# A joint inverse of the 16-blocks by doubling, one block to a partition, with roots and beta products on VectorE

## The chip, the core and the metric

The kernel runs on one core of a Trainium2 chip. The metric is the device time of one execution in microseconds (us). The engines are called by the profile's names: PE (TensorE; PEld is its weight load), DVE (VectorE), ACT (ScalarE), POOL (GpSimd) and SP, whose queue issues the transfers (DMA) spoken of here. Each engine executes its instructions in the order in which they were placed on it.

## What is computed

One inference step of a hybrid recurrent decoder of one layer, for 1024 prompt tokens and 8 x 4 sample tokens, in fp32. Cut to what matters:

```
h = RMSNorm(x);  z = h @ w_in
A: gated DeltaNet   o = delta rule over chunks of 64: solve (I + L) sol = rhs, L strictly lower
                    y = o * rsqrt(mean(o*o) + eps) * g * silu(z)
B: RWKV-7           S_t = S_t-1 diag(w) + (S_t-1 (-kk)) (kk*a)^T + v k^T,  o_t = S_t r_t
                    y = group_norm(o) + bonus, times a gate
C: Griffin RG-LRU
x = x + sum_b(sigmoid(gate_b) * (y_b @ w_branch[b])) @ w_out
x = x + relu(RMSNorm(x) @ w_up)^2 @ w_down;   final RMSNorm
```

Both recurrences of A and B are computed in chunks of 64 tokens. Each chunk needs the inverse of a unit triangular 64x64 matrix. It is built from the inverses of its four diagonal 16x16 blocks, then of 32x32, then of 64x64 blocks.

## The kernel before

**Stages.** From the start to about 360 us the first projections run, from there to about 1300 us the middle stage, then the branches are merged and the last GEMMs run. All large products (GEMMs) are computed in three passes of a high and a low half, in `mm3` (lines L306, L307, L308), 352 tokens at a time. Their weights come by 256 KB loads on SP (L291); ACT makes the high half whi (L296), and in the middle stage POOL makes the low half wlo (L297).

**The loop of the middle stage.** Eighteen turns (L1305 to L1325), nine segments for each of two halves of the heads. A turn has a part of branch B, the generator `rwkv_seg` (ur), and one of branch A, `gdn_seg` (ug), and is pipelined by one turn: `next(ur)` prepares B's chunk (decays, reciprocal, the products BK of beta times k, GM from BK and AR); `tri` inverts the matrices of the turn before; `chain` runs the products that use them, and ends with the norms; `next(ug)` prepares A's matrix LA (L1208); `inv16` inverts the 16-blocks. The projections and gates of later columns are in the same program, and a static scheduler, which runs when the program is built, interleaves everything into one order for each engine. GEMMs lie in PE's order between the small matmuls of the loop.

**inv16 (L771 to L794).** It treats six 64x64 matrices together (nt = 6, four of GM, two of LA; four in the turns with B's sample segment). Eight DMAs write the diagonal blocks of GM to DRAM (L781), eight those of LA (L782), a block's row being 64 bytes. One load (L784) brings them back as i16b, each group's blocks repeated on 16 partitions: 128 partitions of 1536 numbers, 768 KB. Then DVE runs fifteen steps of a column recurrence, each a product (L792) and a reduction (L793). The result u16 lies with the rows on the partitions, as `tri` needs it. POOL copies the unit columns in advance (L789, L790).

**tri (L802).** It spreads u16 into ixt (L799), transposes it (L820, tile ix), and begins its matmuls with L824.

**The roots.** `rsqrt` (L579) computes 1/sqrt by a guess on the bits and three Newton steps: on V (DVE) 10 operations, on P (POOL) 13. The root of branch B's group norm (tiles nwyr, nwtr, called at L1110, used on DVE at L1111) and that of branch A's norm (nwyo, nwto, called at L1288, used on ACT at L1291 to scale oa) are on POOL. The one of the q/k norms (nwyg) is on DVE.

**Beta products.** BK's two halves, from kk and from zk, are made by L962: kk's two operations on POOL, zk's two on DVE.

Of the kernel before, what the change touches and what calls it, by code (L numbers as in the profile page):

```python
# [366 lines left out]
def build(tc, ap):  # L367
    nc = tc.nc
    with ExitStack() as ctx:
        k = K(tc, ctx, ap)  # L370
# [208 lines left out]
        def rsqrt(x, shape, tag, E):  # L579

            yi = k.tile(mp, shape, "nwy" + tag, 2, I32)
            t = k.tile(mp, shape, "nwt" + tag, 1)
            E.tensor_scalar(out=yi, in0=x.bitcast(I32), scalar1=-0.5, scalar2=1597463007.0, op0=ALU.mult, op1=ALU.add)
            y = yi.bitcast(F32)
            for _ in range(3):
                E.tensor_tensor(out=t, in0=y, in1=y, op=ALU.mult)
                if E is V:
                    E.scalar_tensor_tensor(out=t, in0=t, scalar=-0.5, in1=x, op0=ALU.mult, op1=ALU.mult)
                    E.scalar_tensor_tensor(out=y, in0=t, scalar=1.5, in1=y, op0=ALU.add, op1=ALU.mult)
                else:  # L590
                    E.tensor_tensor(out=t, in0=t, in1=x, op=ALU.mult)
                    E.tensor_scalar(out=t, in0=t, scalar1=-0.5, scalar2=1.5, op0=ALU.mult, op1=ALU.add)
                    E.tensor_tensor(out=y, in0=t, in1=y, op=ALU.mult)
            return y
# [176 lines left out]
        def inv16(J):  # L771
# [3 lines left out]
            dr = tc.dram_tile([128, nt, 16], F32, name=f"scr_i{k.n}")
            for g in range(8):
                x = slice(16 * g, 16 * g + 16)
                q = 16 * (g % 4)  # L780
                S.dma_start(dr[x, 0:nb], GM[x, g // 4, 0:nb, q:q + 16])  # L781
                S.dma_start(dr[x, nb:nt], LA[x, :, 0, 16 * g:16 * g + 16])  # L782
            mb = k.tile(mp, [128, 1536], "i16b", 1)[:, :256 * nt]
            S.dma_start(mb, dr.rearrange("(g k) b c -> g (k b c)", k=16).unsqueeze(1).to_broadcast([8, 16, 256 * nt]))  # L784
            mb = mb.rearrange("p (k b c) -> p k b c", k=16, b=nt)
            e16 = k.c("e16").unsqueeze(1).to_broadcast([128, nt, 16])
# [735 lines left out]
```

## Time and profile before

| | |
|---|---|
| median of 3 runs | 2380.67 us (2380.59 to 2381.06) |
| profiled execution | 2385.66 us |
| its span, first to last instruction | 2383.9 us |
| mean granted clock of TensorE, share of full speed | 0.937 |
| PE busy in the span | 2225.8 us (93%) |
| DVE, ACT, POOL busy | 1214.3, 814.5, 467.2 us |

The times that follow are those of the profiled execution, counted from the start of its span. The granted clock is a share of 2.4 GHz; 0.50 is the lower level, 1.2 GHz. "Idle before" is the time in which an engine had nothing under way ahead of an instruction, and the name behind it is what ended that time. A turn is counted by when its LA is inverted, from 0.

### The profile page before, as it was taken

How to read it: one execution, taken by the hardware profiler on the slowest of the kernel's cores; microseconds unless marked ns; L12 is line 12 of the kernel's file. 1: busy time of each engine (PE TensorE's matmuls, PEld its weight loads, DVE VectorE, ACT ScalarE, POOL GpSimd, SP SyncE). 2: the span in 40 equal slices, each digit the busy share in tenths (PEclk: the TensorE clock that was granted, in tenths of full speed). 3: DMA queues.
4: the chain of work that ended last, by engine and by line, in shares of the span. 5: the costliest groups of instructions: out<-in, count | busy, mean ns of one | idle time of the engine just before them, and what ended most of it. 6: DMA issues, size and time to landing. Idle time of an engine off the chain costs nothing.

```text
span 2383.9 us, 43121 instructions
## 1 busy us (share of the span) xinstructions
PE 2225.8 (93%) x16939; PEld 2077.3 (87%) x16939; DVE 1214.3 (51%) x2904; ACT 814.5 (34%) x1917; POOL 467.2 (20%) x979
## 2 busy tenths in 40 slices
PE   8999998889888988888978999999999999999997
PEld 7988997678777776777768999999999999999997
DVE  7454347566666675665542037656343333433437
ACT  6465344333433433343322221344122121221234
POOL 3013232432334334223322200032000000000003
PEclk9999998788988897898889999999999999999999
DMA  4213333232323243223223354431111111111114
GB/s 139 71 55 113 102 106 103 80 80 71 88 73 103 67 112 85 78 73 82 68 74 105 121 172 160 158 96 63 45 45 45 49 46 48 45 47 43 49 47 151
DMA packets 149011, 200.15 MB, mean 84 GB/s; under 512 B 36676, under 2 KB 89284, under 8 KB 148808
## 3 DMA queue, kind: packets, MB, share of 16 engines
q1 hardware_dynamic: 148808, 197.40, 27.5%
q8 instruction: 133, 2.18, 0.4%
q14 instruction: 70, 0.57, 0.1%
HBM read 152.61 MB, written 44.72 MB: 83 GB/s over the span
## 4 chain that ended last, share of the span: by engine, by line
PE 55%; DVE 5%; POOL 4%; issue 2%; DMA 2%; ACT 1%; SPq 0%; DVEq 0%; POOLq 0%; ACTq 0%
PE g L306 16%; PE g L307 16%; PE g L308 16%; DVE i16t L792 1%; DMA i16b<-scr_i 1%; PE sr L1041 1%; DVE i16u L793 1%; PE rr L976 1%; POOL wlo L297 0%; PE rg L1204 0%; POOL BK L962 0%; PE sr L1116 0%; DVE ahi L1502 0%; PE sg L1238 0%; PE rr L824 0%
## 5 line engine op out<-in xcount | busy, mean ns | idle before, releaser
L306 PE MATMUL g<-hhi,whi 128*128 128x352 f32 x2568 | 861.8, 336 | 7.7 <-DVE z L360 7.1
L308 PE MATMUL g<-hhi,wlo 128*128 128x352 f32 x2568 | 858.6, 334 | 1.7 <-POOL wlo L297 1.7
L307 PE MATMUL g<-hlo,whi 128*128 128x352 f32 x2472 | 828.8, 335 | 2.6 <-DVE hlo L499 1.6
L306 PEld LDWEIGHTS g<-hhi,whi 128*128 128x128 f32 x2568 | 499.6, 195 | 16.9 <-DVE z L360 8.3
L308 PEld LDWEIGHTS g<-hhi,wlo 128*128 128x128 f32 x2568 | 499.5, 195 | 10.1 <-issue 2.3
L307 PEld LDWEIGHTS g<-hlo,whi 128*128 128x128 f32 x2472 | 482.0, 195 | 11.3 <-DVE hlo L499 2.7
L296 ACT CAST whi<-wraw 128x512 fp32r<-128x512 f32 x326 | 201.2, 619 | 522.5 <-PE g L307 498.7
L308 PE MATMUL g<-ahi,wlo 128*128 128x352 f32 x768 | 248.4, 323 | 0.0
L306 PE MATMUL g<-ahi,whi 128*128 128x352 f32 x768 | 248.4, 323 | 0.0
L307 PE MATMUL g<-alo,whi 128*128 128x352 f32 x768 | 248.1, 323 | 0.0
L297 DVE TENSOR_TENSOR wlo<-wraw,whi 128x512 fp32r<-128x512 f32 x216 | 151.4, 701 | 163.5 <-ACT whi L296 158.6
L297 POOL TENSOR_TENSOR wlo<-wraw,whi 128x512 fp32r<-128x512 f32 x110 | 148.4, 1350 | 349.4 <-ACT whi L296 332.3
L1423 POOL TENSOR_TENSOR acc<-acc,sq 128x352 f32<-128x352 f32 x36 | 36.9, 1026 | 910.5 <-ACT sq L1422 744.6
L1484 DVE TENSOR_TENSOR x<-g,x 128x352 f32<-128x352 f32 x192 | 100.4, 524 | 201.1 <-PE g L308 201.1
L308 PEld LDWEIGHTS g<-ahi,wlo 128*128 128x128 f32 x768 | 144.8, 189 | 0.1
L306 PEld LDWEIGHTS g<-ahi,whi 128*128 128x128 f32 x768 | 144.6, 188 | 0.2
L307 PEld LDWEIGHTS g<-alo,whi 128*128 128x128 f32 x768 | 144.6, 188 | 0.1
L1473 DVE TENSOR_TENSOR rl<-rl,g 128x352 f32<-128x352 f32 x96 | 49.8, 519 | 131.0 <-ACT rl L1472 131.0
L792 DVE TENSOR_TENSOR i16t<-i16u,i16b 128x6 f32<-128x6 f32 (+5 forms) x270 | 84.2, 312 | 28.6 <-DMA i16b<-scr_i 21.7
L1472 ACT ACTIVATE rl<-g 128x352 f32<-128x352 f32 x96 | 44.4, 463 | 136.2 <-PE g L308 136.2
L1475 DVE TENSOR_TENSOR alo<-rl,ahi 128x352 fp32r<-128x352 f32 x96 | 50.4, 525 | 47.5 <-ACT ahi L1474 47.5
L1356 ACT ACTIVATE z<-g 128x352 f32<-128x352 f32 x72 | 33.3, 463 | 111.5 <-PE g L308 111.0
(361 smaller groups left out, 2995.1 us busy)
## 6 DMA issues: line engine op xcount, KB each, us to landing
wraw<-win SPq DMA_DIRECT2D x126, 256.0 KB
wraw<-wdn SPq DMA_DIRECT2D x80, 256.0 KB
wraw<-wup SPq DMA_DIRECT2D x64, 256.0 KB
scr_t<-z SPq DMA_DIRECT2D x24, 528.0 KB
tgl<-scr_t SPq DMA_DIRECT2D x24, 528.0 KB
i16b<-scr_i SPq DMA_DIRECT2D x16, 768.0 KB
scr_za<-z SPq DMA_DIRECT2D x16, 528.0 KB
wraw<-wout SPq DMA_DIRECT2D x32, 256.0 KB
```

The source lines that it names most:

```text
L296: self.A.copy(hi, r3)
L297: self.lo_eng.tensor_tensor(out=lo, in0=r3, in1=hi.bitcast(F32), op=ALU.subtract)
L306: T.matmul(ps, whi(k), xhi(k), start=start and k == ks[0], stop=False)
L307: T.matmul(ps, whi(k), xlo(k), start=False, stop=False)
L308: T.matmul(ps, wlo(k), xhi(k), start=False, stop=stop and k == ks[-1])
L792: V.tensor_tensor(out=t[:, :, 0:c], in0=u[:, :, 0:c], in1=mb[:, 0:c, :, c].rearrange("p k b -> p b k"), op=ALU.mult)
L1356: A.activation(out=tz[:, gl(g)], in_=ps, func=AF.Tanh, scale=0.5)
L1423: (V if last else P).tensor_tensor(out=acc[g], in0=acc[g], in1=sq, op=ALU.add)
L1472: A.activation(out=rl, in_=ps, func=AF.Relu)
L1473: V.tensor_tensor(out=rl, in0=rl, in1=ps, op=ALU.mult)
L1475: V.tensor_tensor(out=b[:, gl(g)], in0=rl, in1=a[:, gl(g)].bitcast(F32), op=ALU.subtract)
L1484: V.tensor_tensor(out=x2[c][:, gl(g)], in0=ps, in1=x2[c][:, gl(g)], op=ALU.add)
```

## The change

**The inverse.** `inv16` becomes two functions. `inv16_load` writes the diagonal 64x64 blocks whole, with two DMAs for GM and two for LA, into one DRAM tile whose blocks are 64 x 64 + 64 numbers apart; so the 16x16 diagonal blocks lie at one stride and one load fetches them: 48 partitions (8 nt), one block of 256 numbers to a partition, in runs of 64 bytes. `inv16_solve` inverts all blocks at once by doubling: unit diagonal, then 2x2, 4x4, 8x8, 16x16, where each step fills the corner R between two inverted blocks with a11 M a22, on DVE, in 17 operations. Its result Z is written to DRAM (one DMA) and read back as u16 (two DMAs), in the layout that `tri` reads. POOL sets Z to the unit matrix ahead of it.

**The roots and products.** `rsqrt` loses its POOL form; every root is ten operations on DVE. Both halves of BK are on DVE, four operations.

```diff
-        def rsqrt(x, shape, tag, E):
+        def rsqrt(x, shape, tag):
...
-                E.tensor_tensor(out=t, in0=y, in1=y, op=ALU.mult)
-                if E is V:
-                    E.scalar_tensor_tensor(out=t, in0=t, scalar=-0.5, in1=x, op0=ALU.mult, op1=ALU.mult)
...
+                V.tensor_tensor(out=t, in0=y, in1=y, op=ALU.mult)
+                V.scalar_tensor_tensor(out=t, in0=t, scalar=-0.5, in1=x, op0=ALU.mult, op1=ALU.mult)
+                V.scalar_tensor_tensor(out=y, in0=t, scalar=1.5, in1=y, op0=ALU.add, op1=ALU.mult)
...
-            for g in range(8):
-                x = slice(16 * g, 16 * g + 16)
-                q = 16 * (g % 4)
-                S.dma_start(dr[x, 0:nb], GM[x, g // 4, 0:nb, q:q + 16])
-                S.dma_start(dr[x, nb:nt], LA[x, :, 0, 16 * g:16 * g + 16])
-            mb = k.tile(mp, [128, 1536], "i16b", 1)[:, :256 * nt]
-            S.dma_start(mb, dr.rearrange("(g k) b c -> g (k b c)", k=16).unsqueeze(1).to_broadcast([8, 16, 256 * nt]))
...
+            w = 64 * 64 + 64
+            dr = tc.dram_tile([2 * nt * w], F32, name=f"scr_i{k.n}")
+            for h in range(2):
+                d = dr[h * nt * w:(h + 1) * nt * w].rearrange("(b x) -> b x", b=nt)[:, 0:64 * 64].rearrange("b (p t) -> p b t", t=64)
+                S.dma_start(d[:, 0:nb], GM[H[h], h, 0:nb, 0:64])
+                S.dma_start(d[:, nb:nt], LA[H[h], :, 0, 64 * h:64 * h + 64])
+            M = J["M"] = k.tile(mp, [48, 272], "i16m", 1)[:8 * nt]
+            src = dr.rearrange("(g x) -> g x", g=8 * nt)[:, 0:16 * 64].rearrange("g (k t) -> g k t", t=64)[:, :, 0:16]
+            S.dma_start(M[:, 0:256], src)
+
+        def inv16_solve(J):
...
+            P.memset(Z, 0.0)
+            P.memset(Z[:, 0:272:17], 1.0)
...
+            V.tensor_copy(Z[:, 1:256:34], M[:, 1:256:34])
...
+            V.tensor_copy(R_, blocks(M, 2, 0, 2))
+            V.tensor_tensor(out=t2, in0=R_[:, :, :, 0], in1=a22.unsqueeze(2).to_broadcast([r, 4, 2]), op=ALU.mult)
+            V.tensor_tensor(out=R_[:, :, :, 1], in0=R_[:, :, :, 1], in1=t2, op=ALU.add)
+            V.tensor_tensor(out=t2, in0=R_[:, :, 1], in1=a11.unsqueeze(2).to_broadcast([r, 4, 2]), op=ALU.mult)
+            V.tensor_tensor(out=R_[:, :, 0], in0=R_[:, :, 0], in1=t2, op=ALU.add)
+
+            def product(out, a, b, n):
...
+                for i in range(m):
+                    V.tensor_tensor(out=p_[:, i], in0=a[:, i].unsqueeze(2).to_broadcast([r, n, n, n]),
+                                    in1=b[:, i].rearrange("p k c -> p c k").unsqueeze(1).to_broadcast([r, n, n, n]), op=ALU.mult)
+                if len(out.shape) == 2:
+                    V.tensor_reduce(out=out, in_=pr_[:, :m * n * n * n].rearrange("p (x k) -> p x k", k=n), axis=AXX, op=ALU.add)
+                    return
+                for i in range(m):
+                    V.tensor_reduce(out=out[:, i], in_=p_[:, i], axis=AXX, op=ALU.add)
+
+            for n in (4, 8):
+                t = tt[:, :8 * n]
+                product(t, blocks(M, n, 0, n), blocks(Z, n, n, n), n)
+                product(blocks(Z, n, 0, n), blocks(Z, n, 0, 0), t.rearrange("p (i r c) -> p i r c", r=n, c=n), n)
+            k.n += 1
+            dr = tc.dram_tile([2, nt, 64, 16], F32, name=f"scr_i{k.n}")
+            S.dma_start(dr.rearrange("h b (q k) c -> (h b q) (k c)", q=4), Z[:, 0:256])
             u = k.tile(mp, [128, 6, 16], "i16u", 2)[:, :nt]
-            t = k.tile(mp, [128, 6, 16], "i16t", 2)[:, :nt]
-            P.tensor_copy(u[:, :, 0:1], e16[:, :, 0:1])
-            P.tensor_copy(t, e16)
-            for c in range(1, 16):
-                V.tensor_tensor(out=t[:, :, 0:c], in0=u[:, :, 0:c], in1=mb[:, 0:c, :, c].rearrange("p k b -> p b k"), op=ALU.mult)
-                V.tensor_reduce(out=u[:, :, c], in_=t[:, :, 0:c + 1], axis=AXX, op=ALU.add)
+            for h in range(2):
+                S.dma_start(u[H[h]], dr[h].rearrange("b p c -> p b c"))
...
-                for src, j, e in ((kk, 0, P), (zk, 1, V)):
+                for src, j, e in ((kk, 0, V), (zk, 1, V)):
...
-                rs = rsqrt(mv[:, 1], [128, nb], "r", P)
+                rs = rsqrt(mv[:, 1], [128, nb], "r")
...
-                rs = rsqrt(oss[:n, :nb], [n, nb], "o", P)
+                rs = rsqrt(oss[:n, :nb], [n, nb], "o")
...
-            inv16(J)
+            inv16_load(J)
+            inv16_solve(J)
```

Lines of the kernel after that are spoken of: the way there is L776, L777 and L780, the solve L792 and L803 to L820, the way back L828 and L831; the root's operations are still L583 to L588, ixt is L837, BK L1000, GM L1017, and L1111 and L1293 of before are L1149 and L1331.

**The order on DVE, turn 12.** Before, behind the reciprocal: k L1111 takes the group norm's root nwyr from POOL, then come the last of B's preparation and the first recurrence steps (i16t, i16u), with gtm and GM between them.

```order
L955 RECIPROCAL k_1653_10550<-k_1653_10550 128x256
L964 TENSOR_TENSOR zr_10518<-zr_10518,par 128x256
L1111 TENSOR_TENSOR k_1596_10255<-k_1596_10255,nwyr_10322 128x256
L1293 SCALAR_TENSOR_TENSOR zg_9895<-sg_10510,d_hang,zg_9895 128x256
L956 TENSOR_TENSOR k_1652_10549<-k_1652_10549,k_1653_10550 128x256
L959 TENSOR_TENSOR zk_10519<-zk_10519,WA_10528 128x256
L962 TENSOR_TENSOR BK_10527<-zk_10519,k_1650_10544 64x4x64 x2
L1120 TENSOR_TENSOR k_1608_10347<-k_1608_10347,zv_9582 128x256
L965 TENSOR_TENSOR zr_10518<-zr_10518,zk_10519 128x256
L792 TENSOR_TENSOR i16t_10432<-i16u_10431,i16b_10429 128x6
L1241 SCALAR_TENSOR_TENSOR gtm_10942<-sg_10944,sc,kv_10365 128x128
L793 TENSOR_REDUCE i16u_10431<-i16t_10432 128x6
```

After, at the same place on DVE, the first half of the solve (i16z, i16t) stands among the operations of the two roots (nwto, nwyo, nwtr, nwyr), ahead of the reciprocal.

```order
L1147 TENSOR_SCALAR mv_10021<-mv_10021 128x4
L792 COPY i16z_10122<-i16m_10120 48x8
L803 COPY i16z_10122<-i16m_10120 48x4x2x2
L583 TENSOR_SCALAR nwyr_10028<-mv_10021 128x4
L587 SCALAR_TENSOR_TENSOR nwto_10180<-nwto_10180,oss_10150 128x2
L804 TENSOR_TENSOR i16t_10126<-i16z_10122 48x8
L586 TENSOR_TENSOR nwtr_10029<-nwyr_10028 128x4
L588 SCALAR_TENSOR_TENSOR nwyo_10179<-nwto_10180,nwyo_10179 128x2
L805 TENSOR_TENSOR i16z_10122<-i16z_10122,i16t_10126 48x4x2
```

Further on, still on DVE after, the end of the solve and what stands between it and ixt.

```order
L814 TENSOR_TENSOR i16p_10125<-i16z_10122,i16t_10126 48x512
L997 TENSOR_TENSOR zk_10200<-zk_10200,WA_10209 128x256
L820 TENSOR_REDUCE i16z_10122<-i16p_10125 48x8x8
L1000 TENSOR_TENSOR BK_10208<-k_1691_10230,k_1689_10225 64x4x64 x2
L1000 TENSOR_TENSOR BK_10208<-zk_10200,k_1689_10225 64x4x64 x2
L1002 TENSOR_TENSOR zr_10199<-zr_10199,par 128x256
L1279 SCALAR_TENSOR_TENSOR gtm_10601<-sg_10603,sc,kv_10068 128x128
L1003 TENSOR_TENSOR zr_10199<-zr_10199,zk_10200 128x256
L1279 SCALAR_TENSOR_TENSOR gtm_10601<-sg_10603,sc,kv_10068 128x128
L1017 TENSOR_TENSOR GM_10256<-rr_10257,con 128x512
L1017 TENSOR_TENSOR GM_10256<-rr_10258,con 128x512
L837 TENSOR_TENSOR ixt_10276<-i16u_10146,con 128x192
```

The solve moved ahead of BK and GM, and these moved between its end and ixt; no operation waits for POOL's nwyr or nwyo any more.

**The order on SP's queue, turn 12.** Before: the eight writes of LA, loads of other parts of the turn, one weight load, and the broadcast i16b.

```order
L782 DMA scr_i_10412<-LA_10364 16x2x16 x8
L1167 DMA gr_11302<-scr_g 128x128 x2
L291 DMA wraw_13855<-win 128x512
L784 DMA i16b_10429<-scr_i_10412 128x1x1536
L902 DMA ll_10998<-scr_l 128x2x128
```

After: the two writes of LA (L777) are followed by one weight load and a load of gr; then come the load i16m, other loads, the stores of both norms' results (scr_y), the write of Z (i16z) and its read (i16u).

```order
L780 DMA i16m_10120<-scr_i_10115 48x16x16
L1205 DMA gr_10955<-scr_g 128x128
L1398 DMA scr_t<-z_13306 128x1056
L291 DMA wraw_13583<-win 128x512
L940 DMA ll_10654<-scr_l 128x2x128
L938 DMA zv_10201<-scr_zb_91 128x2x128
L1161 DMA scr_y<-k_1644_10050 128x128 x2
L1334 DMA scr_y<-zg_9623 128x128 x2
L1211 DMA kq_10958<-scr_za_93 128x2x128 x2
L828 DMA scr_i_10144<-i16z_10122 48x256
L1213 DMA zg_10511<-scr_za_93 128x2x128
L831 DMA i16u_10146<-scr_i_10144 64x6x16 x2
```

The queue has one more round trip in each turn, and its last part stands behind the stores of the norms' results.

**The order on PE.** Between the first and the last of tri's first matmuls (L824, after L862) PE's order holds 1885 GEMM matmuls (L306 to L308) before and 1981 after, of 10584 in both.

## Rows read from the trace of the kernel before

**Rows 1.** windows: length; PE, PEld, DVE, ACT, POOL busy (count); clock; DMA
```profile
360.00:1300.00 940.00, 819.63 (x8321) 693.00 (x8320) 564.78 (x1782) 339.52 (x1048) 307.41 (x759) 0.86 0.31 84
1300.00:2384.00 1084.00, 1064.52 (x6614) 1059.90 (x6612) 469.99 (x829) 292.07 (x549) 69.54 (x61) 0.99 0.25 80
```

**Rows 2.** waits of PE from 360 to 1300 us (total, times, longest)
```profile
PE sg L1292 <- ACT oa L1291: 40.8, 16, 4.9
PE sr L1116 <- DVE k L1111: 25.9, 12, 5.3
PE rr L824 <- DVE ix L820: 23.2, 9, 5.6
```

**Rows 3.** tri's first matmul, line L824 (ns min/median/max, first and last start)
```profile
L824 PE MATMUL rr<-ix,GM x544: 184/191/258, 390.8 to 1253.7; 32*32 32x32 f32 x182
```

**Rows 4.** timeline of DVE, turn 12 (start, duration, operation, idle before)
```profile
973.26 0.47 DVE L1208 SCALAR_TENSOR_TENSOR LA<-rg,gsl,ar 128x256 f32<-128x256 f32 x1
...
981.00 0.17 DVE L1109 TENSOR_SCALAR mv<-mv 128x4 f32<-128x4 f32 x1
981.08 1.74 DVE L955 RECIPROCAL k<-k 128x256 f32<-128x256 f32 x1
...
989.32 0.43 DVE L1111 TENSOR_TENSOR k<-k,nwyr 128x256 f32<-128x256 f32 x1 [6.22 <-POOL nwyr L593]
...
1004.87 0.32 DVE L792 TENSOR_TENSOR i16t<-i16u,i16b 128x90 f32<-128x90 f32 x1
...
1005.51 0.36 DVE L799 TENSOR_TENSOR ixt<-i16u,con 128x192 f32<-128x192 f32 x1
```

**Rows 5.** timeline of POOL, turn 12: where the first root begins
```profile
980.55 0.19 POOL L583 TENSOR_SCALAR nwyo<-oss 128x2 int32<-128x2 int32 x1
```

**Rows 6.** timeline of PE, turn 12
```profile
989.89 1.12 PE L1116 MATMUL sr<-con,k 64*64 64x64 f32 x16 [3.71 <-DVE k L1111]
...
1007.94 0.45 PE L824 MATMUL rr<-ix,GM 32*32 32x32 f32 x32
```

**Rows 7.** windows, the stretch behind PE's stop in turn 12
```profile
985.90:1003.00 17.10, 13.39 (x74) 11.79 (x73) 10.52 (x34) 2.39 (x6) 5.22 (x13) 0.50 0.34 85
```

**Rows 8.** timeline of DVE, turn 13
```profile
1022.03 0.87 DVE L1208 SCALAR_TENSOR_TENSOR LA<-rg,gsl,ar 128x256 f32<-128x256 f32 x2
...
1028.18 1.75 DVE L955 RECIPROCAL k<-k 128x256 f32<-128x256 f32 x1
...
1068.33 0.87 DVE L1208 SCALAR_TENSOR_TENSOR LA<-rg,gsl,ar 128x256 f32<-128x256 f32 x2
```

**Rows 9.** timeline of PE, turn 13
```profile
1050.81 0.65 PE L824 MATMUL rr<-ix,GM 32*32 32x32 f32 x32 [2.01 <-DVE ix L820]
```

**Rows 10.** timeline of SP's queue, first turn
```profile
368.49 0.67 SPq L784 DMA_DIRECT2D i16b<-scr_i  x1
```

**Rows 11.** timeline of DVE, first turn
```profile
378.85 0.17 DVE L792 TENSOR_TENSOR i16t<-i16u,i16b 128x6 f32<-128x6 f32 x1 [2.94 <-DMA i16b<-scr_i]
```

**Rows 12.** chain that ended last: two loads in it (start, duration)
```profile
943.64 2.41 DMA zk<-scr_zb
...
1034.38 3.05 DMA kq<-scr_za
```

**Rows 13.** groups of instructions by form (count; busy us, mean ns; idle before)
```profile
L976 PE MATMUL rr<-AR,BK 64*128 64x128 f32 x272 | 50.2, 354 | 10.9 <-POOL BK L962 9.8 <-ACT og L970 1.1
...
L962 DVE TENSOR_TENSOR BK<-zk,k 64x256 f32<-64x256 f32 x32 | 22.8, 714 | 0.7
...
L979 DVE TENSOR_TENSOR GM<-rr,con 128x512 f32<-128x512 f32 x32 | 21.8, 685 | 14.2 <-PE rr L976 14.2
...
L586 DVE TENSOR_TENSOR nwtg<-nwyg 128x2 f32<-128x2 f32 x48 | 8.4, 175 | 1.0
...
L963 DVE TENSOR_TENSOR AR<-zr,k 128x256 f32<-128x256 f32 x16 | 7.8, 484 | 0.4 <-ACT k L936 0.4
...
L1104 DVE TENSOR_REDUCE mv<-k 128x4 f32<-128x256 f32 x16 | 6.5, 409 | 0.0
```

More of the change, by code (lines that the diff above doesn't have):

```diff
@@ L577, in b4 @@
             return a.rearrange("p (b w) -> p b w", b=NB)
-        def rsqrt(x, shape, tag, E):
+        def rsqrt(x, shape, tag):
             yi = k.tile(mp, shape, "nwy" + tag, 2, I32)
             t = k.tile(mp, shape, "nwt" + tag, 1)
-            E.tensor_scalar(out=yi, in0=x.bitcast(I32), scalar1=-0.5, scalar2=1597463007.0, op0=ALU.mult, op1=ALU.add)
+            V.tensor_scalar(out=yi, in0=x.bitcast(I32), scalar1=-0.5, scalar2=1597463007.0, op0=ALU.mult, op1=ALU.add)
             y = yi.bitcast(F32)
             for _ in range(3):
-                E.tensor_tensor(out=t, in0=y, in1=y, op=ALU.mult)
-                if E is V:
-                    E.scalar_tensor_tensor(out=t, in0=t, scalar=-0.5, in1=x, op0=ALU.mult, op1=ALU.mult)
[L589 to L593, printed above, removed]
+                V.tensor_tensor(out=t, in0=y, in1=y, op=ALU.mult)
+                V.scalar_tensor_tensor(out=t, in0=t, scalar=-0.5, in1=x, op0=ALU.mult, op1=ALU.mult)
+                V.scalar_tensor_tensor(out=y, in0=t, scalar=1.5, in1=y, op0=ALU.add, op1=ALU.mult)
             return y
@@ L769, in build, with inv16_load @@
         H = [slice(0, 64), slice(64, 128)]
[L771 removed]
+        def inv16_load(J):
             GM, LA, nb, nt = J["GM"], J["LA"], J["nb"], J["nb"] + 2
             k.n += 1
[L777 to L793 removed]
@@ new lines, in inv16_load, with blocks @@
+            S.dma_start(M[:, 0:256], src)
+        def inv16_solve(J):
+            nt = J["nb"] + 2
+            r = 8 * nt
+            M = J["M"]
+            Z = k.tile(mp, [48, 272], "i16z", 2)[:r]
+            P.memset(Z, 0.0)
+            P.memset(Z[:, 0:272:17], 1.0)
+            pr_ = k.tile(mp, [48, 512], "i16p", 1)[:r]
+            tt = k.tile(mp, [48, 64], "i16t", 1)[:r]
+            V.tensor_copy(Z[:, 1:256:34], M[:, 1:256:34])
+            def blocks(a, n, row, col):
+                o = 16 * row + col
+                a = a.rearrange("p (i x) -> p i x", x=34 * n)[:, :, o:o + 16 * n]
+                return a.rearrange("p i (r t) -> p i r t", t=16)[:, :, :, 0:n]
+            R_, a11, a22 = blocks(Z, 2, 0, 2), blocks(Z, 2, 0, 0)[:, :, 0, 1], blocks(Z, 2, 2, 2)[:, :, 0, 1]
+            t2 = tt[:, 0:8].rearrange("p (i c) -> p i c", c=2)
+            V.tensor_copy(R_, blocks(M, 2, 0, 2))
[4 more added lines that the diff above has]
+            def product(out, a, b, n):
+                m = 8 // n
+                p_ = pr_[:, :m * n * n * n].rearrange("p (i r c k) -> p i r c k", i=m, r=n, c=n)
+                for i in range(m):
[13 more added lines that the diff above has]
+            S.dma_start(dr.rearrange("h b (q k) c -> (h b q) (k c)", q=4), Z[:, 0:256])
+            u = k.tile(mp, [128, 6, 16], "i16u", 2)[:, :nt]
+            for h in range(2):
+                S.dma_start(u[H[h]], dr[h].rearrange("b p c -> p b c"))
@@ L1190, in gdn_seg @@
                 V.tensor_scalar(out=ss, in0=ss, scalar1=0.25, scalar2=EPS, op0=ALU.mult, op1=ALU.add)
-                rk = rsqrt(ss[:, 0], [n, nb], "g", V)
+                rk = rsqrt(ss[:, 0], [n, nb], "g")
                 sl = k.tile(mp, [128, 3, 2], "gsl", 2)[:n]
```

## The prediction

> **What bounds the kernel now.** I read the profile by stage first. From 360 to 1300 us the kernel runs eighteen turns of the two recurrent branches. PE is busy for 819.6 of those 940 us, at a mean granted clock of 0.86; after 1300 us it is busy for 1064.5 of 1084 us at 0.99 [rows 1]. So the last 1084 us are PE's own and nothing in this change touches them. The middle has 120 us in which PE is idle and a good deal more in which it runs at its lower level: 819.6 busy us at 0.86 would be about 705 at full clock, so 235 us stand open there.
>
> Then I asked what PE waits for in that stage. Three waits make up 90 of the 120 us: on oa (the gated norm's root, scaled by ACT), on k at L1111 (the group norm's root) and on ix (the inverse of the 16-blocks, turned for tri) [rows 2]. Two are the roots that POOL computes, one is the inverse itself, and all three are what the change rewrites.
>
> Third, I followed one turn. tri's first matmul comes at 390.8 us in the first turn and for the last time at about 1253.7, which is 17 turns of 50.8 us [rows 3]. A turn is a loop: the evacuation of LA on DVE, the inverse, tri on PE, the chain products and the next LA. In turn 12 LA is done at 973.26 + 0.47 = 973.73 [rows 4] and tri starts at 1007.94 [rows 6]: 34.2 us. From there to the next LA, done at 1022.03 + 0.87 = 1022.90 [rows 8], it takes 15.0 us. In turn 13 the first part takes 1050.81 - 1022.90 = 27.9 us [rows 8, 9] and the second 1069.20 - 1050.81 = 18.4 us. The change works in the first part.
>
> What fills the 34.2 us: DVE works through some twenty operations of both branches until 981.17, does a reciprocal, and then sits idle for 6.22 us until POOL's second root is there at 989.3; POOL began the first root at 980.55 and runs the two one behind the other [rows 4, 5]. Then come the products and thirty steps of the column recurrence, until ixt at 1005.51 [rows 4]. PE, waiting for k, is idle for 3.71 us at 989.89 [rows 6], and in the 17.1 us from 985.9 it is granted 0.50, its 1.2 GHz level [rows 7]. So the root costs twice: in DVE's wait, and in PE's clock after it.
>
> **The change, part by part, for LA to tri of turn 12.**
> (a) Work that stays ahead of the solve's end. 973.73 to 981.17 stays, 7.4 us. The reciprocal (1.74) and five 128x256 operations that now stand between the solve's steps (L1111, zg, L956, L959, L1120 of before) stay too; one takes 0.43 [rows 4], and back to back a little less, say 0.36. That is 1.74 + 1.8 = 3.6.
> (b) The roots. Twenty small DVE operations take the place of 26 on POOL. One takes 0.175 [rows 13]. Alone in a dependent row they come every 0.2 us, 4.0 in all; interleaved, as they are now, with another dependent row, they may come every 0.1, 2.0 in all. I take 3.0. The 6.22 us wait and POOL's two hops go.
> (c) The solve. Seventeen operations on 48 partitions. Six on 8 to 16 elements, 0.2 each, 1.2. Four products of 64 elements at 0.16 to 0.32, where the L792 step of 90 elements took 0.32 [rows 4], say 0.25, and three reductions at 0.22: 1.7. Two products of 512 elements: at least 0.69, as L979's [rows 13]; at most about 1.1, if each element costs what L792's did beyond a small operation's 0.16 ((0.32 - 0.16)/90 = 1.8 ns); 0.85. Two reductions of 512 elements: 0.41 for 256 in L1104 [rows 13], at most double; 0.68. The last four are 3.1. Together 6.0, with ends of 5.0 and 6.9.
> (d) The way back, which is new: the result is written to DRAM and read into u16 before tri can use it. Before, only the way there existed. The nearest rows are two loads of the kernel that stand in the chain, 2.41 and 3.05 us [rows 12]. Two legs of that size and their issues (0.4 and 0.8, as of one and two DMAs) are 6.0 to 7.3; I take 6.7. The far row is the broadcast of before: issued at 368.49, used at 378.85, 10.4 us [rows 10, 11]; that is the upper end, for a rival below. What hides under it: the four beta products, zr, gtm and GM, which DVE now has between the solve and ixt.
> (e) ixt, the transpose and the start of tri: 2.4 us in turn 12 (1005.51 to 1007.94), 0.9 at best with PE free; 1.2.
> Sum: 7.4 + 3.6 + 3.0 + 6.0 + 6.7 + 1.2 = 27.9, against 34.2: 6.3 us less. Turn 13: until the reciprocal DVE needs 1028.18 - 1022.90 = 5.3 [rows 8], then the second reduction and its scaling 0.5, and the same rest: 5.3 + 0.5 + 3.6 + 3.0 + 6.0 + 6.7 + 1.2 = 26.3 against 27.9: 1.6 less. The mean of the two is 4.0.
>
> The way there costs nothing in this sum: the small load is issued behind two LA writes instead of eight. From 973.7, with two issues (0.9), a landing of 2.4 to 3.05, an issue of 0.6 and a load of the same size, it is there 6.3 to 7.6 us later, where DVE reaches the solve 7.4 us after LA. If that cover goes, it costs up to 2 us in turns like the thirteenth. On SP the load stands behind one weight load (L291, between L777 and L780), and a wait there holds every load behind it; the Z write stands behind the two stores of scr_y and kq's loads, which are due some 2 us before the solve ends.
>
> Beta products: two more on DVE. The two it has take 0.714 each while POOL does its two, and L963, as many elements a partition, 0.484 [rows 13]. Four of them lie between 1.9 and 2.9 us, under the way back; their cost shows only where GM becomes late. By the Trainium skill (SBUF — State Buffer, Who interferes with whom) a DVE instruction with two SBUF inputs and a GpSimd one that reads SBUF share a read port and block each other. These rows agree (0.714 against 0.484); by that rule the four would cost 1.9 us, which is the lower of those two ends.
>
> **Whole kernel.** 17 turns of 4.0 are 68 us. The second part of a turn took 15.0 and 18.4; with shorter idle stretches ahead of it I give back 1.0 of the mean 1.7, 17 us. The order holds 1885 GEMM matmuls between the first and the last tri before and 1981 after: 96 leave the stage behind it, where 6614 matmuls took 1064.5 us, 0.16 each [rows 1], 15 us. Together 100. The profiled execution took 2385.7 us (span 2383.9), 5.0 above the median. 2385.7 - 100 - 5.0 = 2280.7.
>
> **Rivals.** First, DVE becomes the bound (17%). It executes in order and gets the roots, two beta products and the solve. If beta products stay at 0.714, GM comes after 2.9 us of them, 1.4 us of zr and gtm, some 3.0 us of L976 on PE (50.2 us in 17 turns [rows 13]) and two evacuations of 0.69: 8.7 us, and at half clock 10. ixt stands behind GM on DVE, so 2 to 3 us of each turn's 4.0 go, and the clock gives nothing back: 17 x 0.9 + 15 = 30, so 2350. For it: DVE is already busy for 564.8 of the 940 us [rows 1], 31 a turn. Against it: some 3 us a turn of that time is idle on POOL's root, in which it does nothing.
> Second, the one on the slower side (8%): transfers of short runs are slow. The load of M reads 64-byte runs, 768 of them, and the read into u16 is of 64-byte runs too. If that last leg takes 10.4 us, as the broadcast did [rows 10, 11], the way back is 0.4 + 2.7 + 0.8 + 10.4 = 14.3 in place of 6.7, and turns are 7.6 - 4.0 = 3.6 longer: 61 lost, 15 won in the tail, 2385.7 + 46 - 5 = 2427. It decides from a way back of about 12 us (6.7 + 4.0 + the tail's share of 0.9). Against it: the broadcast moved 768 KB, this leg 48 KB in two. The Trainium skill speaks for it: DMA: Bandwidth & Descriptors, Specifications, asks for at least 512 B a transfer for line rate and says that shorter ones do a read-modify-write. No row here shows what that costs a load of this size.
> Third, the stage recovers its clock (10%): with no root to wait for, PE stays at its upper level, and two thirds of the 235 open us come back: about 160, so 2220.
> Fourth, the change gives nothing (3%): tri waits for a GEMM or for a load blocked on SP as long as before, and the time stays at 2381.
>
> **How the numbers follow.** The forecast, 62%, is 2280. Its own range: the bounds of (b), (c), (d) and (e) hardly go one way together; half of their sum is about 2 us a turn, 34 us, and the clock's share goes from 0 to 29: 2234 to 2331. For 8 in 10 it reaches up to the first rival and down to the third: 2220 to 2355. Some 0.2% can be told from no change by measurement. Faster by more: 0.62 + 0.17 + 0.10 = 0.89; within it 0.03; slower 0.08.
>
> **What would show it.** In the profile after: a turn, tri to tri, of about 45.8 us (50.8 - 5.0); no wait of DVE or ACT on POOL's nwyr or nwyo; LA to tri near 27; the solve's seventeen operations in some 6 us beyond what stands between them; the wait of ixt on the read of u16 a few us, with DVE idle there 0 to 3 us; fewer matmuls after the last tri. I am wrong on (d) if that wait is over 5 us in most turns, on (b) if the roots' rows take 4 us or more, on the first rival's side if ixt starts right behind GM with u16 long there, and on the way there if L792's copy waits for i16m.

## The result, and the profile after

The kernel after takes 2242.3 us, median of 4 runs (2237.6 to 2253.5), against 2380.6 before: a ratio of 0.943, 95% interval 0.939 to 0.947, or 138 us less. The forecast was 2280 with a range of 2220 to 2355. The profiled execution took 2237.6 us (span 2235.8).

First the stages, as in [rows 1], cut at the last turn's tri (length; busy time and count of PE, PEld, DVE, ACT, POOL; granted clock; DMA share; GB/s); the third row is LA to tri of turn 12:

```profile
360.00:1120.00 760.00, 710.18 (x8004) 598.48 (x8004) 567.13 (x1903) 329.61 (x1021) 185.90 (x253) 0.98 0.31 87
1120.00:2235.80 1115.80, 1090.18 (x6954) 1080.62 (x6954) 484.37 (x879) 301.99 (x576) 73.90 (x65) 0.99 0.25 81
897.30:921.70 24.40, 21.85 (x180) 19.37 (x180) 21.96 (x77) 12.38 (x36) 6.92 (x8) 1.00 0.39 102
```

PE is still the busiest engine, but the clock of the middle stage is 0.98 where it was 0.86, and turn 12 runs at 1.00 where the stretch of [rows 7] had 0.50. After the last tri there are 1115.8 us; before, 2383.9 - 1253.3 = 1130.6. tri's first matmul, as in [rows 3], and the waits of PE, as in [rows 2]:

```profile
L862 PE MATMUL rr<-ix,GM x544: 184/191/258, 390.2 to 1120.2; 32*32 32x32 f32 x182
```

```profile
PE sr L1154 <- DVE i16z L820: 7.3, 4, 2.4
PE rr L862 <- DVE ix L858: 7.3, 9, 1.4
PE sr L1154 <- DVE k L1149: 6.3, 7, 1.6
...
PE sg L1330 <- ACT oa L1329: 5.3, 5, 2.0
```

A turn is now (1120.0 - 390.2)/17 = 42.9 us, 7.8 less. The three waits of [rows 2], 89.9 us, have become 26.2 in these four lines (sr's wait on DVE now stands under two names, i16z and k); a third line of sr's, behind nwto, has 2.0 more. No engine waits for a root on POOL, since there is none.

Turn 12 on DVE (start, duration, operation, idle before), as in [rows 4]:

```profile
896.84 0.48 DVE L1246 SCALAR_TENSOR_TENSOR LA<-rg,gsl,ar 128x256 f32<-128x256 f32 x1
...
903.46 1.24 DVE L583 TENSOR_SCALAR nwyo<-oss 128x2 int32<-128x2 int32 x1
...
905.69 0.15 DVE L1147 TENSOR_SCALAR mv<-mv 128x4 f32<-128x4 f32 x1
905.76 0.15 DVE L792 COPY i16z<-i16m 48x8 f32<-48x8 f32 x1
905.83 0.16 DVE L803 COPY i16z<-i16m 48x16 f32<-48x16 f32 x1
905.91 0.15 DVE L583 TENSOR_SCALAR nwyr<-mv 128x4 int32<-128x4 int32 x1
905.98 0.14 DVE L587 SCALAR_TENSOR_TENSOR nwto<-nwto,oss 128x2 f32<-128x2 f32 x1
...
908.92 0.15 DVE L588 SCALAR_TENSOR_TENSOR nwyo<-nwto,nwyo 128x2 f32<-128x2 f32 x1
908.99 1.75 DVE L993 RECIPROCAL k<-k 128x256 f32<-128x256 f32 x1
...
910.98 1.02 DVE L814 TENSOR_TENSOR i16p<-i16m,i16z 48x512 f32<-48x512 f32 x1
...
912.32 0.67 DVE L817 TENSOR_REDUCE i16t<-i16p 48x64 f32<-48x512 f32 x1
...
913.25 1.14 DVE L814 TENSOR_TENSOR i16p<-i16z,i16t 48x512 f32<-48x512 f32 x1
...
914.62 0.70 DVE L820 TENSOR_REDUCE i16z<-i16p 48x64 f32<-48x512 f32 x1
...
918.22 1.28 DVE L1017 TENSOR_TENSOR GM<-rr,con 128x512 f32<-128x512 f32 x2
920.78 0.36 DVE L837 TENSOR_TENSOR ixt<-i16u,con 128x192 f32<-128x192 f32 x1 [1.29 <-DMA i16u<-scr_i]
```

LA is done at 897.32. The solve begins at 905.76, in the middle of the roots; by 908.99 all twenty root operations and the first thirteen of the solve are through. The four operations on 512 elements end at 915.32. Then come the beta products, zr, gtm and GM, and ixt waits 1.29 us more for u16. On SP's queue the way there is L780 and the way back L828 and L831, and tri starts on PE:

```profile
901.54 0.37 SPq L780 DMA_DIRECT2D i16m<-scr_i  x1
...
915.58 0.41 SPq L828 DMA_DIRECT2D scr_i<-i16z  x1
...
917.49 1.28 SPq L831 DMA_DIRECT2D i16u<-scr_i  x2
```

```profile
921.70 0.42 PE L862 MATMUL rr<-ix,GM 32*32 32x32 f32 x29 [0.31 <-DVE ix L858]
```

LA to tri: 921.70 - 897.32 = 24.4 us, against 34.2 before. Turn 13 is another case:

```profile
955.08 0.79 SPq L1161 DMA_DIRECT2D scr_y<-k  x2
955.96 0.38 SPq L828 DMA_DIRECT2D scr_i<-i16z  x1
956.45 0.52 SPq L1213 DMA_DIRECT2D zg<-scr_za  x1
957.06 1.70 SPq L1211 DMA_DIRECT2D kq<-scr_za  x2
958.81 0.46 SPq L1205 DMA_DIRECT2D gr<-scr_g  x1
959.37 1.28 SPq L831 DMA_DIRECT2D i16u<-scr_i  x2
```

```profile
952.95 0.67 DVE L820 TENSOR_REDUCE i16z<-i16p 48x64 f32<-48x512 f32 x1
...
962.48 0.36 DVE L837 TENSOR_TENSOR ixt<-i16u,con 128x192 f32<-128x192 f32 x1 [3.54 <-DMA i16u<-scr_i]
```

The solve ends at 953.62, but SP issues the store of k first, for which POOL's last product had to be done, so Z is written at 955.96; its read stands behind the loads of zg, kq and gr and is issued at 959.37. The way back takes 962.48 - 953.62 = 8.9 us, against 5.5 in turn 12, and DVE idles for 3.54 of them.

### The profile page after: what moved, and what is told of

Read it like the earlier page. It is cut to its first block, busy times and chain, and to the rows that moved or that the text cites. A ratio compares the mean times of both kernels' runs of the same rounds, so it can differ in the third digit from the quotient of the medians.

```text
span 2235.8 us, 42651 instructions
## 1 busy us (share of the span) xinstructions
PE 2141.0 (96%) x16939; PEld 2001.6 (90%) x16939; DVE 1226.2 (55%) x3066; ACT 814.1 (36%) x1917; POOL 348.0 (16%) x475
## 5 line engine op out<-in xcount | busy, mean ns | idle before, releaser
L306 PE MATMUL g<-hhi,whi 128*128 128x352 f32 x2568 | 850.8, 331 | 16.1 <-DVE z L360 10.7
L308 PE MATMUL g<-hhi,wlo 128*128 128x352 f32 x2568 | 844.3, 329 | 1.7 <-POOL wlo L297 1.7
L307 PE MATMUL g<-hlo,whi 128*128 128x352 f32 x2472 | 813.8, 329 | 3.5 <-DVE hlo L499 2.3
L306 PEld LDWEIGHTS g<-hhi,whi 128*128 128x128 f32 x2568 | 488.4, 190 | 28.9 <-DVE z L360 13.3
L308 PEld LDWEIGHTS g<-hhi,wlo 128*128 128x128 f32 x2568 | 488.2, 190 | 8.9 <-POOL wlo L297 2.3
L307 PEld LDWEIGHTS g<-hlo,whi 128*128 128x128 f32 x2472 | 471.3, 191 | 13.3 <-DVE hlo L499 3.8
L308 PE MATMUL g<-ahi,wlo 128*128 128x352 f32 x768 | 248.4, 323 | 0.0
L306 PE MATMUL g<-ahi,whi 128*128 128x352 f32 x768 | 248.4, 323 | 0.0
L297 POOL TENSOR_TENSOR wlo<-wraw,whi 128x512 fp32r<-128x512 f32 x110 | 153.9, 1401 | 368.5 <-ACT whi L296 348.3
L308 PEld LDWEIGHTS g<-ahi,wlo 128*128 128x128 f32 x768 | 144.8, 189 | 0.1
L306 PEld LDWEIGHTS g<-ahi,whi 128*128 128x128 f32 x768 | 144.6, 188 | 0.2
L1512 DVE TENSOR_TENSOR rl<-rl,g 128x352 f32<-128x352 f32 x96 | 49.8, 518 | 133.7 <-ACT rl L1511 133.7
L1511 ACT ACTIVATE rl<-g 128x352 f32<-128x352 f32 x96 | 44.3, 462 | 138.7 <-PE g L308 138.7
L1513 ACT CAST ahi<-rl 128x352 fp32r<-128x352 f32 x96 | 46.7, 487 | 63.2 <-DVE rl L1512 63.2
```

The lines of the kernel that those rows point to most:

```text
L297: self.lo_eng.tensor_tensor(out=lo, in0=r3, in1=hi.bitcast(F32), op=ALU.subtract)
L306: T.matmul(ps, whi(k), xhi(k), start=start and k == ks[0], stop=False)
L307: T.matmul(ps, whi(k), xlo(k), start=False, stop=False)
L308: T.matmul(ps, wlo(k), xhi(k), start=False, stop=stop and k == ks[-1])
L1511: A.activation(out=rl, in_=ps, func=AF.Relu)
L1512: V.tensor_tensor(out=rl, in0=rl, in1=ps, op=ALU.mult)
```

## The experiments

Fourteen kernels were compared, before and after among them. "Idle" is the span of the profiled execution less PE's busy time. "Low" is the time at the lower level, worked out from the mean granted clock, which has two levels: 2 x (1 - clock) x span. "LA to tri", from the end of LA's second evacuation on DVE to tri's first matmul, is the mean of the eighteen turns, and "turn" a seventeenth of the time between the first and the last tri, both from the timelines. A ratio stands against runs of the kernel before in the same session, whose median lay between 2371 and 2381 us.

| kernel | inverse | roots | kk's beta | median us | ratio, 95% | PE busy | idle | low | LA to tri | turn |
|---|---|---|---|---|---|---|---|---|---|---|
| before | old | POOL | POOL | 2380.6 | 1 | 2225.8 | 158.1 | 300 | 35.6 | 50.7 |
| roots | old | DVE | POOL | 2353.1 | 0.990 (0.987 to 0.993) | 2216.7 | 137.0 | 264 | 33.8 | 49.1 |
| rootsbeta | old | DVE | DVE | 2341.0 | 0.987 (0.981 to 0.992) | 2203.1 | 145.3 | 235 | 34.4 | 49.8 |
| inverse | new | POOL | POOL | 2332.9 | 0.983 (0.979 to 0.987) | 2185.6 | 143.5 | 200 | 35.4 | 48.9 |
| after_rootspool | new | POOL | DVE | 2328.3 | 0.981 (0.977 to 0.985) | 2196.4 | 131.5 | 219 | 34.5 | 48.8 |
| after_betapool | new | DVE | POOL | 2261.0 | 0.953 (0.948 to 0.957) | 2156.7 | 101.7 | 113 | 30.5 | 44.3 |
| after | new | DVE | DVE | 2242.3 | 0.943 (0.939 to 0.947) | 2141.0 | 94.8 | 85 | 28.6 | 42.9 |

**The parts of the change, alone and together.** Four kernels each take one part, or leave one out, and one more completes the old inverse's side. Only the calls are shown; the functions go with them.

```diff
roots, rootsbeta (against before)
-                rs = rsqrt(mv[:, 1], [128, nb], "r", P)
+                rs = rsqrt(mv[:, 1], [128, nb], "r", V)
-                rs = rsqrt(oss[:n, :nb], [n, nb], "o", P)
+                rs = rsqrt(oss[:n, :nb], [n, nb], "o", V)
rootsbeta too, after_rootspool (against inverse); after_betapool (against after) the other way
-                for src, j, e in ((kk, 0, P), (zk, 1, V)):
+                for src, j, e in ((kk, 0, V), (zk, 1, V)):
inverse (against before)
-            inv16(J)
+            inv16_load(J)
+            inv16_solve(J)
```

> The kernel before with one part of the change alone: the roots of both norms on DVE (10 operations instead of 13 on POOL), the old inverse, kk's beta products on POOL. Root theory (the wait on POOL's roots and PE's half clock behind it carry the gain): half of the 138 us or more, so 2310 us or less, and the granted clock of the middle stage goes from 0.86 to 0.93 or more. Inverse theory (the two trips' length and the thirty column steps carry it): DVE reaches the recurrence some 3 us earlier and then waits for the broadcast i16b, which still comes some 20 us after LA; 20 to 30 us, so about 2355, and DVE's wait on i16b goes from 21.7 us to 50 or more.

> The kernel before with the new inverse alone; both roots and kk's beta products stay on POOL. Root theory: the 3 us wait on the root in each turn and the half clock stay, the gain is what the shorter inverse gives beside them, 60 us or less, so 2320 or more, and the middle stage's clock stays under 0.92. Inverse theory: 90 us or more, so 2290 or less, since LA to tri loses the broadcast and the column steps.

> The kernel after with the two roots back on POOL and all else as it is (new inverse, four beta products on DVE). Root theory: 60 us or more come back, 2300 or more, with waits of DVE on nwyr of 3 us a turn and PE's clock under 0.93. Inverse theory: the root's 8.7 us on POOL now lie beside a solve that does not need them, and 30 us or less come back, 2272 or less.

> The kernel after with kk's beta products back on POOL. My step (the four products lie under the way back and cost nothing there): the time stays within 8 us of 2242. Rival, the products on DVE delay GM and with it ixt: without them it is 15 us or more faster, 2227 or less. Second rival, POOL's copies were the slow part (0.87 us each, with a hop between engines, and PE waited 9.8 us for them): it gets 10 us or more slower, 2252 or more.

> The kernel before with the roots and kk's beta products on DVE and the old inverse: the last corner of the eight combinations that bears on the change. If the beta products gain by themselves, as they gain 19 us beside the new inverse and the DVE roots: 20 us under the 2353 of the roots alone, 2333. If they gain only where the turn is short enough for GM to matter: 2348 to 2358, no gain beside the old inverse, as they gave 5 us beside POOL's roots.

Neither theory holds alone. The roots by themselves give 21 us, as the inverse theory said; the inverse by itself gives 41, as the root theory said; and the kernel after with its roots back on POOL (after_rootspool) loses 86, again as the root theory said. Together (after_betapool) the two parts give 113, 51 more than the sum. The waits show why. In the run of the roots, DVE's longest wait is the broadcast (total, times, longest). It was 21.7 us in 6 turns before; the 50 that the inverse theory named was not reached:

```profile
DVE i16t L792 <- DMA i16b<-scr_i: 44.3, 15, 4.8
```

In the run of the inverse DVE still waits for the root, longer than before (55.1 us in 18 turns), and PE with it:

```profile
DVE k L1154 <- POOL nwyr L593: 65.8, 18, 6.4
DVE ixt L842 <- DMA i16u<-scr_i: 55.7, 14, 6.3
```

```profile
PE sg L1335 <- ACT oa L1334: 45.3, 15, 7.0
PE sr L1159 <- DVE k L1154: 20.1, 10, 3.8
```

and in its turn 12 that wait lies inside the solve:

```profile
957.62 0.16 DVE L797 COPY i16z<-i16m 48x8 f32<-48x8 f32 x1
...
965.99 1.46 DVE L1154 TENSOR_TENSOR k<-k,nwyr 128x256 f32<-128x256 f32 x1 [6.00 <-POOL nwyr L593]
...
977.22 0.67 DVE L825 TENSOR_REDUCE i16z<-i16p 48x64 f32<-48x512 f32 x1
```

The first row is the start of the solve, the last its last reduction: 20.3 us, of which 6.00 are the root's. With the old inverse the recurrence could not begin before the broadcast had landed, and the root's wait lay in part under that; with the new one the data are there early, and since DVE works in order, a root that comes late holds up the rest of the solve. Each part leaves the wait that the other removes, and lengthens it: the broadcast's from 21.7 to 44.3 us, the root's from 55.1 to 65.8.

The beta products were expected to lie hidden (within 8 us) or to get in the way. They did neither: the change loses 19 us without them, the second rival of that run, while they give 12 us beside the old inverse and 5 beside POOL's roots (in both cases the two intervals overlap). So that they gain is shown only for the whole. PE's waits for BK are 14.1 us without them and 5.7 with them, which fits the hop to POOL as what they save, but is only part of the 19; the rest is argued, not shown. A rival stands untested for all differences of this size: the scheduler orders every kernel anew, so that they can be those of the order and not of the part.

**How much of the turn reaches the time.** Five kernels change the loop after. The first leaves the last corners of the inverse unfilled, so its results are not those of the program.

```diff
no_n8
-            for n in (4, 8):
+            for n in (4,):
way_twice, behind the write of Z
+            d2 = tc.dram_tile([2, nt, 64, 16], F32, name=f"scr_j{k.n}")
+            S.dma_start(d2.rearrange("h b p c -> (h b p) c"), dr.rearrange("h b p c -> (h b p) c"))
+            dr = d2
write16
+                for q in range(0, 64, 16):
+                    x = slice(64 * h + q, 64 * h + q + 16)
+                    S.dma_start(d[q:q + 16, 0:nb, q:q + 16], GM[x, h, 0:nb, q:q + 16])
+                    S.dma_start(d[q:q + 16, nb:nt, q:q + 16], LA[x, :, 0, 64 * h + q:64 * h + q + 16])
way_act (the same for the write of Z)
-                S.dma_start(u[H[h]], dr[h].rearrange("b p c -> p b c"))
+                A.dma_start(u[H[h]], dr[h].rearrange("b p c -> p b c"))
one_read
-            dr = tc.dram_tile([2, nt, 64, 16], F32, name=f"scr_i{k.n}")
+            dr = tc.dram_tile([nt, 2, 64, 16], F32, name=f"scr_i{k.n}")
...
+            S.dma_start(u, dr.rearrange("b h p c -> (h p) b c"))
```

> The kernel after without the last doubling step (n = 8) of the solve: its two products of 512 elements and two reductions, some 3.2 us of DVE in each turn, and the corner that they fill stays zero, so the 16-blocks are not inverted whole. If the DVE stretch from LA to the Z write still sets the turn, 3.2 us come off most of the 17 turns: 35 to 55 us, so 2188 to 2207. If PE is the bound by now (93% busy at a clock of 0.98 in the stage), at most 20 us: 2222 or more.

> The kernel after with a copy from DRAM to DRAM put between the write of Z and its read, so that the way back has one leg more: some 0.4 us of issue and 1.7 to 2.3 us of landing. If the way back is on the path in the 12 turns in which ixt waits for i16u now, and soon in the others: 17 times 2.5, some 40 us, 2280 or so. If it lies under the beta products and GM: 10 us or less, 2252 or less. My prediction held that it decides from a way back of about 12 us.

> The kernel after with the blocks written to DRAM by sixteen small DMAs in each turn, as before, instead of four; the tile, the one load of M and all else are unchanged. SP's issue of the LA writes takes 3.6 us instead of 0.9 to 1.3, so i16m lands some 2.5 us later than DVE reaches the solve, 7.9 us after LA in the median. If that cover is as thin as my sum held: 17 times some 2 us, less what PE no longer lets through, so 15 to 35 us slower, 2257 to 2277. If the small transfers are free because DVE comes later than they do: within 6 us of 2242.

> The kernel after with the write of Z and the two reads of u16 issued on ACT's queue instead of SP's. In turn 13 the write is issued 2.4 us after the solve ends, behind the store of k, and the read behind kq and gr: the way back took 8.9 us, against 5.5 in turn 12. If SP's order costs that, the turns like 13 win 2 to 3 us: 10 to 25 us faster, 2217 to 2232. If ACT, which now waits for Z's landing ahead of its own work (whi, the scaling of oa), hands the loss on to PE: 10 us or more slower, 2252 or more.

> The kernel after with the halves next to each other in both DRAM tiles, so that u16 comes back in one DMA of 128 partitions instead of two of 64: one issue of 0.6 us less in the way back and on SP. If each microsecond of the way back counts: 0.6 in each turn, 10 us faster, 2232. If PE is the bound by now: within 4 us of 2242.

| kernel | median us | ratio, 95% | PE busy | idle | low | LA to tri | turn |
|---|---|---|---|---|---|---|---|
| no_n8 | 2235.6 | 0.940 (0.935 to 0.944) | 2145.6 | 75.2 | 98 | 25.7 | 40.3 |
| way_twice | 2261.4 | 0.952 (0.949 to 0.955) | 2159.1 | 99.8 | 122 | 33.2 | 47.2 |
| write16 | 2253.3 | 0.950 (0.945 to 0.955) | 2158.8 | 92.1 | 122 | 32.5 | 46.9 |
| way_act | 2243.9 | 0.944 (0.941 to 0.947) | 2145.4 | 95.9 | 94 | 28.9 | 43.8 |
| one_read | 2242.7 | 0.943 (0.940 to 0.946) | 2142.8 | 99.4 | 99 | 29.5 | 43.7 |

The solve without its last step has turns 2.6 us shorter, 44 us in 17 turns, and only 7 us of them are seen in the median time (15 in the profiled execution). The windows of no_n8, cut at its last tri, say where they went:

```profile
360.00:1070.00 710.00, 674.36 (x7703) 561.37 (x7700) 502.94 (x1823) 317.62 (x1000) 157.32 (x245) 0.95 0.31 87
1070.00:2220.00 1150.00, 1129.09 (x7233) 1121.00 (x7233) 482.34 (x880) 312.04 (x596) 84.69 (x73) 0.99 0.25 82
```

From 1070 to its end it runs 1150 us, against 1115.8 after the last tri of the kernel after. The GEMMs that no longer find a place in the loop run behind it, at PE's full pace. The other way round, way_twice makes a turn 4.3 us longer, 73 in all, and the time 19 us longer; the copy put the read of u16 3.3 us later behind the write (median 5.6 against 2.3). In write16 the solve starts 12.4 us after LA in the median, against 7.9: the cover of the small way there is as thin as the sum held, and still the time grows by 11 us only, with intervals that overlap. Other queues or one issue less (way_act, one_read) change nothing that can be told from noise. So no_n8 and one_read came out as they should if PE is the bound; way_twice, write16 and way_act lie between the times that their two theories had named, and meet neither. None of these is a better kernel: near the result, a sixth to a quarter of what happens in the loop reaches the time.

**The clock.** At the same 16939 matmuls PE's busy time fell from 2225.8 to 2141.0: 85 of the 148 us of span, beside the 63 that idle time gave. The 85 are those of one pair of executions. The profiled one of before has a clock of 0.937, while the 31 others whose clock is on record have 0.936 to 0.954, with a median of 0.946. In all kernels of the tables busy time goes with the time at the lower level: 0.39 us of it for each us of "low" from after to before (84.8/215), and by that the inverse alone, for one, should have 2141 + 0.39 x 115 = 2186; it has 2185.6, and the others lie within 6 us. At the median clocks of before and after (0.946 and 0.980) the same factor gives, as an estimate, 65 us of PE's time in place of 85: about half of the gain, not most of it. What brings the lower level about was asked with two kernels that add useless work to the kernel before.

```diff
warm (and the same with oa ahead of the other norm)
+                ps = k.tile(pq, [128, 512], "sr", 1)
+                for _ in range(4):
+                    T.matmul(ps[:, 0:64 * nb].rearrange("p (b c) -> p b c", b=nb), k.c("ident"), O, start=True, stop=True)
                 V.tensor_tensor(out=O, in0=O, in1=rs.unsqueeze(2).to_broadcast([128, nb, 64]), op=ALU.mult)
...
warm2 (called with y of the first and of the second Newton step, each in a tile of its own)
+                def fill(y):
+                    for _ in range(3):
+                        T.matmul(ps[0:nb, 0:64 * nb].rearrange("p (b c) -> p b c", b=nb), y, O, start=True, stop=True)
```

> The kernel before with useless work added on PE: four matmuls of 128x256 fp32 ahead of each norm's transposes (their output is overwritten), where PE waits for POOL's roots. At the duration of L951's two (0.70 us for 2) that is 8 x 0.35 = 2.8 us a turn, some 48 us in all. Clock theory (the gain of the change is for the larger part PE's busy time, which fell by 85 us at the same 16939 matmuls, since PE no longer stops and is then granted 0.50): the added work takes the place of idle time and the stage's clock rises from 0.86 to 0.92 or more, so that the time grows by 15 us at most. If the clock has nothing to do with those stops: it stays near 0.86 and the time grows by 35 us or more.

> The kernel before with useless matmuls inside PE's two stops: each root's first and second Newton step on POOL goes to a tile of its own, and PE multiplies each of the two by the 256 columns it waits with, three times (12 matmuls a turn, their output is overwritten). In the run named warm the added matmuls stood ahead of the stops, which stayed (64 us against 67), and the clock stayed too. Here they can run only while the root is on its way. If PE's fall to its lower level comes of these stops: the two waits fall below 35 us, the stage's granted clock rises from 0.86 to 0.91 or more, and in spite of some 80 us of added work (0.40 us each, as in that run) the time stays under 2420. If the level has another cause: the clock stays at 0.88 or less and the time is 2440 or more. If the waits don't fall below 50 us, it tells nothing.

The windows from 360 to 1300 us of warm, then of warm2, and PE's waits at the two norms in each:

```profile
360.00:1300.00 940.00, 825.51 (x8311) 690.87 (x8312) 553.68 (x1790) 330.50 (x1027) 293.83 (x751) 0.87 0.28 78
```

```profile
PE sr L1118 <- DVE k L1114: 33.7, 16, 4.1
PE sg L1297 <- ACT oa L1296: 33.1, 15, 2.7
```

```profile
360.00:1300.00 940.00, 841.40 (x8559) 643.68 (x8560) 553.80 (x1793) 335.90 (x1035) 300.34 (x753) 0.92 0.29 82
```

```profile
PE sr L1121 <- POOL nws0r L597: 26.9, 14, 3.5
PE sg L1304 <- POOL nws0o L597: 21.6, 15, 3.4
```

In warm the work ran ahead of the stops; they stayed (66.8 us), the clock stayed at 0.87, and the time grew by 56 us (ratio 1.023, 1.018 to 1.028). That run could not tell the clock theory apart, because it did not remove what it meant to. In warm2 the work ran inside the stops. Its 432 matmuls are busy for 120 us; the time grew by 45 (1.019, 1.016 to 1.022), the clock rose to 0.92, and without the added work PE is busy for 2160.7 us, 65 less than before for the same matmuls. The rise does not hang on the one profiled execution of before: over whole executions the clock is 0.964 to 0.966 in warm2 and 0.944 to 0.951 in the kernel before of that session, against 0.942 to 0.948 in warm and 0.938 to 0.952 before. The waits at the two norms missed the bound of 35 us set for them: they come to 48.5, and to 54.9 with 6.4 more at the next steps, which is above the 50 from which the run was to tell nothing. They are cut in pieces, though: the longest is 3.5 us where [rows 2] has 4.9 and 5.3. So useless work ahead of the stops left the clock, and useless work inside them raised it: that the stops bring the level down is supported, but not shown. The added work also differs in amount (67 us busy in warm, 120 in warm2), and amount and place were not tried apart. How the level depends on a stop's length these runs don't settle.

## Why the prediction was right, and where its sum was off

Direction and range held, and so did the mechanism as far as it went: the roots' wait is gone, the solve is short, the way there is covered. The gain was 138 where the sum said 100, and the time lies nearer to the third rival's 2220 than to 2280. Point by point:

**LA to tri of turn 12** came out at 24.4, forecast 27.9. Work ahead of the solve: 905.76 - 897.32 = 8.4 for 7.4, because two of the twenty root operations stand in it, and one of these, L583, took 1.24 us. Parts (a, second half), (b) and (c) together: 915.32 - 905.76 = 9.6 for 12.6. The last four operations took 3.3 of it (3.1 forecast), the six operations of 128x256 3.4 (3.6 forecast); but the small ones of roots and solve came to 2.9, or 4.1 with the two root operations ahead of it, for 5.9. That is the term that I mis-sized most: three interleaved rows start every 0.07 us, faster than the 0.10 that was its lower end. The way back (d): 5.5 for 6.7. The start of tri (e): 0.9 for 1.2. Turn 13 came out at 26.7, forecast 26.3, which is luck: the small operations won there too, and SP's order took it back in a way back of 8.9.

**The sample.** From turns 12 and 13 the sum had 4.0 a turn. In these two turns 5.5 came (a mean of 31.0 before and 25.6 after), and over all eighteen 7.0 (35.6 and 28.6). So of the 3.0 that are missing a turn, half is in the sizes above, the small operations above all, and half in the sample: a difference taken over two turns, of which turn 13 was one of the shortest before (27.9). Each half is some 26 us of the sum. The mean itself is pulled up by turns 1 and 10, in which LA comes long before its tri (59.5 and 53.1 before, 46.4 and 36.9 after). The other way went the second part of the turn, where I gave back 1.0 and 0.5 came. In the 17 turns between the first tri and the last the two parts are 7.3 and 0.5; 17 x 7.8 and 15 behind them make the 148 of the span; the medians lie 10 closer.

**Behind the last tri** 15 us were forecast from the 96 GEMMs; 1130.6 - 1115.8 = 14.8.

**The way there** is covered: DVE waits for i16m 2.2 us in 3 turns. **The beta products** end well before u16 is there in turns 12 and 13, and measured 0.60 and 0.42 each (below), 2.0 for four, at the lower of the two ends.

**The first rival** (DVE's order becomes the bound) did not come: GM is done before u16 is there in turns 12 and 13, and ixt waits for u16 33.8 us in 12 turns. Its price was also too high by up to 19 us: it took 0.9 a turn, where 4.0 less 2 to 3 leaves 1 to 2. **The second** (slow short runs) neither: the three new transfers land in 1.7 to 3.0 us in the median. Its point of decision, a way back of 12 us, was also too near: way_twice shows that a turn made longer there costs a quarter of what it grows by. **The third** (the clock recovers) is the one that mostly happened beside the forecast: of 300 us at the lower level 85 are left. I had the clock in the sum with 17 us, as a shorter second part of the turn; it is 65 to 85 us of PE time, most of it within LA to tri, where it sits in the 7.0: of the 300 us some 200 lay there before, and of the 85 some 30 after. Prices by turn and prices by engine are two accounts of the same 148 us, not two gains.

## What to carry to other kernels

Two waits that lie side by side hide each other: price each edit with the other one made, since the pair can give nearly twice the sum of the two. Take the mean turn of a loop from all its turns before multiplying. And where PE is busy for nine tenths, make a second account of the span, busy plus idle: an edit in the loop is worth what it takes from PE's idle time and from its time at the lower level, and the rest moves behind the loop.
